# Another order of tokens, ring loads split around a loop's test, and an expert's odd-shaped matmuls gathered into one run

## The chip, the cores and the metric

One core of one Trainium2 chip runs the whole program. The metric is device time in microseconds (us) of one execution. The core has a matmul engine (PE, whose weight loads are listed as PEld), two elementwise engines (DVE and ACT), a general engine (POOL, idle here), and a sequencer (SP) that issues nearly all transfers. ACT issues a few. All transfers run on the same 16 DMA engines.

## The reference, cut to what matters

Two layers over 256 tokens of 1024 float32 values. Each layer mixes tokens in four branches (neighbourhood attention on a 4 x 64 grid, differential attention, pooling, dilated attention), and then sends each token to 2 of 32 experts:

```python
h = layer_norm(x, emb_ln_g, emb_ln_b)
for l in range(2):
    z = h @ w_in[l]                                  # 1024 x 8192 weights
    ... four branches, gates, merged @ w_out[l] ...
    h = layer_norm(ALPHA * h + mix, ln1_g[l], ln1_b[l])
    # group by argmax, then the top 2 of 8 experts in the group
    # expert e: (silu(t @ w_gate[e]) * (t @ w_up[e])) @ w_down[e], weighted by its gate
    h = layer_norm(ALPHA * h + ffn, ln2_g[l], ln2_b[l])
return h                                             # (1, 256, 1024)
```

An expert's three matrices are 2 MB each. All 32 are read in each layer, 201 MB, whether tokens chose them or not.

## The kernel before, in words

**Tokens.** The kernel keeps the 256 tokens in an order of its own, on two tiles of 128 partitions. Slot `64r + 16b + a` holds token `16a + 4b + r`, so that tokens with the same remainder by 4 lie together, as the dilated branch wants. `x` comes in with four transfers of 64 rows of 4 KB (line 390), and the result leaves with four such transfers, two issued by SP and two by ACT (line 1009). The rows of one transfer are walked as 4 x 16. The neighbourhood branch needs the plain order, so lines 617, 618, 623, 638 and 652 (its `y_store`) read or write through two views, `grid` and `mine`.

**Weights.** `weight_sources` names the blocks of weights in the order in which they are used, and `load_weight` issues the next one whenever a buffer of 1 MB comes free. There are eight buffers that live all through (`rawp`), eight that open with the third branch (`rawb`), and four (`rawc`, the ring) that open with `open_ring` after the output projection, in the room of the tiles `wh` and `wl`. A block of `w_in` that is made of two column ranges of 256 is filled by two transfers per buffer, with pieces of 1 KB; one that is 512 columns wide by one transfer, with pieces of 2 KB.

**Token mixing.** Each weight block is split by ACT (`high`, line 233) and DVE (`low`, line 238) into two parts, and PE makes three passes over them (lines 447, 466 and 759). At the start the program loads `x`, takes its mean and variance (lines 259 to 275), normalises it (290, 292), turns it on PE (346), and scales it by columns of gains (298, 300) that come from two small loads (306), turned on PE (315) and copied by ACT (316). Then the first products begin.

**Experts.** After routing, `overflow` tests whether any expert has more than 64 tokens: every engine loads the number of trips (line 1301) and passes a loop (1302) that runs zero times here. Then the loop of `moe` over 32 experts `p` has twelve steps `s`. Steps 0 to 7 multiply the tokens of expert `p` by its gate and up matrices (843), and free two buffers each at s = 3 and s = 7. Steps 8 to 11 are the down product of expert `p - 1` (867), which frees one buffer at s = 9 and one at s = 11. Beside them, by the table `STEPS`: `combine` adds expert `p - 2` to the sum (888), `turn` transposes the hidden values (853). For the next batch of four experts, `gather` picks token rows by matmul (803), one piece at s = 5 and one at s = 6, and `gathered` copies them out (812). `gather_meta` (820) does the same for token numbers once in four experts. The order of the instructions inside this loop is as written (`manual_schedule`). Outside of such a block, a scheduler decides where an instruction stands on its engine.

**End.** After the last expert the second sum is normalised (259, 999, 1006) and written out (1009).

Of the kernel before, what the change touches and what calls it, by code (L numbers as in the profile page):

```python
# [29 lines left out]
G = 2  # L30
NORM_ON = ((1, 0), (1, 0))
RAW = (4, 2, 4, 4)

STEPS = ((0, 2, "select"), (3, 2, "combine"), (7, 0, "evacuate"), (9, 0, "turn"), (9, 0, "silu"), (9, 0, "times_up"),
         (11, 1, "weigh"))


def token_order():
    p = np.arange(SEQ)
    r, b, a = p // 64, (p // 16) % 4, p % 16  # L40
    return 16 * a + 4 * b + r

# [64 lines left out]
class Kernel:  # L107
# [19 lines left out]
    def open_ring(self):  # L127

        self.close_side()
        self.side = [self.tc.tile_pool(name=f"rawc{self.layer}", bufs=RAW[2] * 2 // G, side="right", reuse_waits="tile")]  # L130
        self.rawc, = (p.__enter__() for p in self.side)
        for _ in range(RAW[2] * 2 // G):
            self.load_weight(self.rawc)
# [11 lines left out]
    def weight_sources(self):  # L145
        a = self.a
        for l in range(self.depth):
# [3 lines left out]
            def cols(*starts, w=w):  # L151
                return [(w[:, :, s:s + 256], 256) for s in starts]

            yield l, [(w[:, :, d:d + 512], 512)]
            yield l, cols(d + 768, d + 1024)
            yield l, cols(d + 1536, d + 1792)
            yield l, cols(d + 512, d + 1280)
# [212 lines left out]
    def run(self):  # L370
        tc, nc, a = self.tc, self.nc, self.a
        with ExitStack() as ctx:
# [14 lines left out]
            h = self.new_h()  # L387
            x = a["x"].rearrange("o (a b r) d -> r b (o a) d", b=4, r=4)
            for r in range(4):
# [43 lines left out]
    def mixing(self, l):  # L433
# [37 lines left out]
        with ExitStack() as ctx:  # L471
# [144 lines left out]

            grid = lambda t: t.rearrange("p (a b r) -> p r b a", b=4, r=4)
            mine = lambda t: t.rearrange("p (r b a) -> p r b a", r=4, b=4)
            ps = crosswise()
# [157 lines left out]
    def moe(self, l):  # L777
        tc, nc, a, c = self.tc, self.nc, self.a, self.c
        mm, t2, t4, t8 = self.mm, self.t2, self.t4, self.t8
        with ExitStack() as ctx:  # L780
# [48 lines left out]
            with tc.tile_pool(name=f"route{l}", bufs=1) as rp:  # L829
                with tc.manual_schedule():  # L830
                    router, xh, xl, acc = self.output_and_route(l, rp, route, meta, slots, gather, gathered)
                self.overflow(l, rp, route, *router, xh, xl, acc)
                gates = router[1]
            work = pool("mwork", 2)
# [59 lines left out]
            with tc.manual_schedule():  # L894
                nc.vector.tensor_copy(meta[:, :, :, 1], gates)
                for p in range(N_EXP):
# [4 lines left out]
                    for s in range(12):  # L901
# [8 lines left out]
                        if p == 0 and s in (1, 3):  # L910
# [3 lines left out]
                            gathered(0, s // 2 + 2, ps, s == 1)  # L914
                        if j == 0 and s == 8:
                            gather_meta(b0, gb)
                            gathered_meta(b0, gb)
                        if e0 < N_EXP and s in (5, 6):
                            gather(e0, 2 * j + s - 5, gb, xh, xl)
                            if s == 6:  # L920
                                gathered(e0, j, gb, False)
                        if s < 8:
                            i = s // 4 * 2
                            products(p, s, tiles[i][:, s % 4], tiles[i + 1][:, s % 4])
                            if s % 4 == 3:
                                free(i)
                                free(i + 1)
                        elif p:
                            down(p - 1, s - 8, tiles[s // 2 - 4][:, s % 2], dn)
                            if s % 2:  # L930
                                free(s // 2 - 4)
                        for at, lag, f in STEPS:
                            if at == s and p >= lag:
                                steps[f](p - lag)
# [58 lines left out]
                else:  # L993
# [8 lines left out]
                    mv = self.norm_stats(0, 1, meanwhile=first)  # L1002
                    o = self.out.rearrange("o (a b r) d -> r b (o a) d", b=4, r=4)
                    for T in range(2):
# [385 lines left out]
```

## Time and profile before

| What | Value |
|---|---|
| median of 3 runs | 1569.12 us (1568.67 to 1569.28) |
| the profiled execution, its own time | 1568.56 us |
| its span | 1566.4 us |
| PE busy | 1486.1 us, 95% |
| DVE, ACT busy | 574.2 us, 465.3 us |
| moved by DMA | 501.14 MB, mean 320 GB/s |
| mixing, layer 0 and layer 1 | about 30 to 303 us, and 791 to 1066 us |
| experts, layer 0 and layer 1 | about 325 to 784 us, and 1085 to 1542 us |

The span is the stretch in which instructions were recorded; 2.2 us of the profiled execution lie outside of it. [...] What a change is worth must be read stage by stage: in the mixing stages PE hardly rests while the DMA engines are partly idle, and in the expert stages the DMA engines are busy without a gap.

### The profile page before, as it was taken

To read this page: it belongs to the slowest core of one execution; us is meant where nothing else is said; L and a number is where in the kernel's file an instruction comes from. 1 tells how busy PE (TensorE), PEld (TensorE's weight loads), DVE (VectorE), ACT (ScalarE), POOL (GpSimd) and SP (SyncE) were. 2 spreads that over 40 slices of the span, in tenths; PEclk is the share of its full clock that TensorE was granted. 3 is DMA by queue.
4 is the path that set the end of the run, shared out by engine and by line. 5 is a ranking of instruction groups with operands and counts; after the bars stand their busy time and mean duration, and the time that the engine had idled before them with its cause. 6 is when DMAs were issued, how large, how long until landed. Compare 5 with 4: busy or idle time off the path is not lost. (4 is left out here: it accounts for less than half of the span.)

```text
span 1566.4 us, 21436 instructions
## 1 busy us (share of the span) xinstructions
PE 1486.1 (95%) x8776; PEld 863.4 (55%) x8776; DVE 574.2 (37%) x1202; ACT 465.3 (30%) x756; POOL 0.2 (0%) x4
## 2 busy tenths in 40 slices
PE   3999999989999999999989999999999999999993
PEld 2787799843334333334468778996333333333342
DVE  3676675721111111111176776664111111111113
ACT  3545554521111111111165455454111111111111
POOL 0000000000000000000000000000000000000000
PEclk9999999999999999999999999999999999999997
DMA  8773386569999999999998246754999999999993
GB/s 221 210 281 108 111 302 207 199 230 420 420 420 419 419 421 419 420 419 420 394 268 287 91 133 209 249 179 187 412 420 420 419 420 421 419 419 421 420 420 124
DMA packets 125785, 501.14 MB, mean 320 GB/s; under 512 B 23082, under 2 KB 44010, under 8 KB 76788
## 3 DMA queue, kind: packets, MB, share of 16 engines
q1 hardware_dynamic: 125400, 499.14, 82.5%
q8 instruction: 71, 1.16, 0.3%
q10 hardware_dynamic: 284, 0.60, 0.1%
q14 instruction: 30, 0.25, 0.0%
HBM read 498.65 MB, written 2.00 MB: 320 GB/s over the span
## 5 line engine op out<-in xcount | busy, mean ns | idle before, releaser
L843 PE MATMUL bank<-raw,xs 128*64 128x512 f32 x2048 | 496.4, 603 | 12.8 <-SPq L1302 5.3
L843 PEld LDWEIGHTS bank<-raw,xs 128*64 128x64 f32 x2048 | 138.5, 136 | 239.2 <-issue 201.5
L867 PE MATMUL bank<-raw,act 128*64 128x512 f32 (+1 forms) x1056 | 247.2, 586 | 0.0
L847 ACT COPY hid<-bank 128x512 f32<-128x512 f32 x64 | 68.4, 1069 | 582.3 <-PE bank L843 582.3
L238 DVE TENSOR_TENSOR wl<-raw,wh 128x1024 fp32r<-128x1024 f32 x160 | 193.7, 1221 | 109.5 <-ACT wh L233 107.9
L233 ACT CAST wh<-raw 128x1024 fp32r<-128x1024 f32 x160 | 166.5, 1048 | 139.1 <-PE mm L466 63.7
L812 DVE COPY xs<-bank 128x256 f32<-128x256 f32 x116 | 43.8, 419 | 343.2 <-PE bank L803 343.2
L466 PE MATMUL mm<-hth,wl 128*128 128x256 f32 x576 | 162.6, 283 | 1.6 <-DVE wl L238 1.6
L466 PE MATMUL mm<-hth,wh 128*128 128x256 f32 x576 | 162.8, 283 | 0.2 <-ACT wh L233 0.2
L466 PE MATMUL mm<-htl,wh 128*128 128x256 f32 x576 | 162.3, 282 | 0.0
L867 PEld LDWEIGHTS bank<-raw,act 128*64 128x64 f32 x1056 | 74.2, 137 | 107.7 <-issue 101.0
L862 DVE TENSOR_TENSOR act<-act,bank 128x256 f32<-128x256 f32 x64 | 27.0, 421 | 265.6 <-ACT act L859 265.6
L466 PEld LDWEIGHTS mm<-hth,wl 128*128 128x128 f32 x576 | 109.2, 190 | 3.1 <-DVE wl L238 1.8
L466 PEld LDWEIGHTS mm<-hth,wh 128*128 128x128 f32 x576 | 109.2, 190 | 2.5 <-issue 2.0
L466 PEld LDWEIGHTS mm<-htl,wh 128*128 128x128 f32 x576 | 109.6, 190 | 0.8 <-issue 0.7
L879 DVE SCALAR_TENSOR_TENSOR y<-bank,tg,y 128x512 fp32r<-128x512 f32 (+1 forms) x66 | 48.5, 735 | 115.4 <-ACT y L878 115.4
L803 PEld LDWEIGHTS bank<-g,xh 128*128 128x128 f32 x240 | 36.2, 190 | 94.9 <-issue 94.9
L447 PE MATMUL mm<-wh,hth 128*128 128x512 f32 x224 | 75.7, 409 | 2.0 <-DVE t L300 1.0
L878 ACT ACTIVATE y<-bank,tg 128x512 fp32r<-128x512 f32 (+1 forms) x66 | 44.5, 674 | 100.5 <-PE bank L867 100.5
L447 PE MATMUL mm<-wl,hth 128*128 128x512 f32 x224 | 73.2, 405 | 0.0
L447 PE MATMUL mm<-wh,htl 128*128 128x512 f32 x224 | 71.5, 401 | 0.0
L803 PE MATMUL bank<-g,xh 128*128 128x256 f32 x240 | 60.7, 335 | 0.0
(220 smaller groups left out, 1420.6 us busy)
## 6 DMA issues: line engine op xcount, KB each, us to landing
raw<-in_expert_w_gate_dram SPq DMA_DIRECT2D x128, 1024.0 KB, 18.2
raw<-in_expert_w_up_dram SPq DMA_DIRECT2D x128, 1024.0 KB, 19.9
raw<-in_expert_w_down_dram SPq DMA_DIRECT2D x124, 1024.0 KB, 19.7
raw<-in_w_in_dram SPq DMA_DIRECT2D x48, 1024.0 KB, 7.5
raw<-in_w_in_dram SPq DMA_DIRECT2D x32, 512.0 KB, 8.7
raw<-in_w_branch_dram SPq DMA_DIRECT2D x8, 1024.0 KB, 4.9
raw<-in_w_out_dram SPq DMA_DIRECT2D x8, 1024.0 KB
raw<-in_expert_w_down_dram SPq DMA_DIRECT2D x16, 256.0 KB, 8.3
```

What stands on the lines that cost most here:

```text
L233: self.nc.scalar.copy(hi, s)
L238: self.nc.vector.tensor_sub(lo, s, raw(hi))
L447: nc.tensor.matmul(ps[T], s[:, kk, T * 128:(T + 1) * 128], m[:, k], stop=kk == 7 and s is stat[1], start=kk == 0 and s is stat[0] and m is wh)
L466: nc.tensor.matmul(ps[j // 2][:, j % 2], m[:, k, j * 128:(j + 1) * 128], s[:, kk], start=j % 2 == 0 and kk == 0 and m is wh and s is hth, ...
L803: nc.tensor.matmul(ps[:, o:o + 256], (xh, xl)[i][:, T, k], gs[e0][:, T], start=i == 0 and T == 0, stop=i == 1 and T == 1)
L812: (nc.scalar.copy if on_scalar else nc.vector.tensor_copy)(xs[e0 + 2 * i][:, :, 2 * j:2 * j + 2], ps[:, 2 * i:2 * i + 2])
L843: nc.tensor.matmul(gu[half[i]], x, w, start=k == 0, stop=k == 7)
L847: nc.scalar.copy(st["h", e].rearrange("q (h k p) -> q h p k", h=2, k=2), gu.rearrange("q (h p k) -> q h p k", h=2, k=2))
L862: nc.vector.tensor_mul(st["a", e], st["a", e], fv[:, :, 1])
L867: nc.tensor.matmul(ps[half[f], :w.shape[2]], st["a", e][:, k], w[:, f], start=k == 0, stop=k == 3)
L878: nc.scalar.activation(yh, ps, AF.Copy, scale=g)
L879: nc.vector.scalar_tensor_tensor(yl, ps, g, raw(yh), op0=ALU.mult, op1=ALU.subtract)
```

## The change

Four edits:

1. Slot `64r + m` now holds token `4m + r`. Each transfer of `x` and of the result is walked as 64 rows. `grid` and `mine` become views of two dimensions, r and m, in place of three.
2. Two blocks of `w_in` per layer, which were two adjacent ranges of 256 columns, are now written as one of 512.
3. `open_ring` fills two of the ring's four buffers, and `load_ring` is called again after the overflow loop for the other two.
4. In the expert loop, both gathers move to s = 9, after the down product of that step; `combine` moves from s = 3 to s = 9, after `turn`; `gather_meta` moves from s = 8 to s = 6.

```diff
-STEPS = ((0, 2, "select"), (3, 2, "combine"), (7, 0, "evacuate"), (9, 0, "turn"), (9, 0, "silu"), (9, 0, "times_up"),
+STEPS = ((0, 2, "select"), (7, 0, "evacuate"), (9, 0, "turn"), (9, 0, "silu"), (9, 0, "times_up"), (9, 2, "combine"),
          (11, 1, "weigh"))
 def token_order():
     p = np.arange(SEQ)
-    r, b, a = p // 64, (p // 16) % 4, p % 16
-    return 16 * a + 4 * b + r
+    return 4 * (p % 64) + p // 64
...
-        for _ in range(RAW[2] * 2 // G):
+        self.load_ring()
+
+    def load_ring(self):
+
+        for _ in range(RAW[2] // G):
             self.load_weight(self.rawc)
...
-            yield l, cols(d + 768, d + 1024)
-            yield l, cols(d + 1536, d + 1792)
+            yield l, [(w[:, :, d + 768:d + 1280], 512)]
+            yield l, [(w[:, :, d + 1536:d + 2048], 512)]
...
-            x = a["x"].rearrange("o (a b r) d -> r b (o a) d", b=4, r=4)
+            x = a["x"].rearrange("o (m r) d -> r (o m) d", r=4)
...
-            grid = lambda t: t.rearrange("p (a b r) -> p r b a", b=4, r=4)
-            mine = lambda t: t.rearrange("p (r b a) -> p r b a", r=4, b=4)
+            grid = lambda t: t.rearrange("p (m r) -> p r m", r=4)
+            mine = lambda t: t.rearrange("p (r m) -> p r m", r=4)
...
                 self.overflow(l, rp, route, *router, xh, xl, acc)
+                self.load_ring()
...
-                        if j == 0 and s == 8:
+                        if j == 0 and s == 6:
                             gather_meta(b0, gb)
                             gathered_meta(b0, gb)
-                        if e0 < N_EXP and s in (5, 6):
-                            gather(e0, 2 * j + s - 5, gb, xh, xl)
-                            if s == 6:
-                                gathered(e0, j, gb, False)
...
+                        if e0 < N_EXP and s == 9:
+                            for k in range(2):
+                                gather(e0, 2 * j + k, gb, xh, xl)
+                            gathered(e0, j, gb, False)
...
-                    o = self.out.rearrange("o (a b r) d -> r b (o a) d", b=4, r=4)
+                    o = self.out.rearrange("o (m r) d -> r (o m) d", r=4)
```

What the four edits move on the engines can be seen in the built programs. The first place is the start of SP's queue, before and then now; the size behind a transfer is the shape that it is walked in.

```order
L390 DMA h<-in_x_dram 64x1x1024 x4
L215 DMA raw<-in_w_in_dram 128x4x512 x2
L407 DMA cs<-in_const_small_dram 128x898
L215 DMA raw<-in_w_in_dram 128x4x256 x12
L417 DMA rpb_141<-in_na_rpb_dram 64x1860
```

```order
L394 DMA h<-in_x_dram 64x1024 x4
L219 DMA raw<-in_w_in_dram 128x4x512 x2
L411 DMA cs<-in_const_small_dram 128x898
L219 DMA raw<-in_w_in_dram 128x4x512 x4
L219 DMA raw<-in_w_in_dram 128x4x256 x4
L421 DMA rpb_137<-in_na_rpb_dram 64x1860
```

The rows of `x` lost an inner dimension, and eight transfers of 256 columns became four of 512. Nothing changed places.

The second place is SP's queue around the loop's test in layer 0, before and then now, with the buffers' numbers, which follow the order in which the code asks for them (`tripsi` is the number of trips).

```order
L197 DMA raw_3044<-in_expert_w_gate_dram 128x2048
L197 DMA raw_3046<-in_expert_w_up_dram 128x2048
L200 DMA raw_3048<-in_expert_w_down_dram 128x2048
L200 DMA raw_3050<-in_expert_w_down_dram 128x2048
L1301 TENSOR_LOAD tripsi_3227
L1301 ISA x2
L1019 DMA rw_5955<-in_router_group_w_dram 128x8x4
L1302 COMPARE_AND_BRANCH
```

```order
L201 DMA raw_3040<-in_expert_w_gate_dram 128x2048
L201 DMA raw_3042<-in_expert_w_up_dram 128x2048
L204 DMA raw_3393<-in_expert_w_down_dram 128x2048
L204 DMA raw_3395<-in_expert_w_down_dram 128x2048
L1306 TENSOR_LOAD tripsi_3219
L1306 ISA x2
L1024 DMA rw_5947<-in_router_group_w_dram 128x8x4
L1307 COMPARE_AND_BRANCH
```

The two loads that are now asked for behind the loop (3393 and 3395, numbers above that of `tripsi`) still stand ahead of the test on SP: the scheduler put them there. The same holds in layer 1.

The third place is PE at the last expert of a layer, before and then now: `raw,xs` are the gate and up products, `raw,act` the down products, `cs,hid` the transposes, `y,sel` the combining.

```order
L843 MATMUL bank<-raw,xs 64x512 x8
L888 MATMUL at<-y,sel 128x512 x4
L888 MATMUL mm<-y,sel 128x512 x4
L843 MATMUL bank<-raw,xs 64x512 x8
L867 MATMUL bank<-raw,act 64x512 x4
L853 MATMUL bank<-cs,hid 128x128 x4
L867 MATMUL bank<-raw,act 64x512 x4
```

```order
L848 MATMUL bank<-raw,xs 64x512 x16
L872 MATMUL bank<-raw,act 64x512 x4
L858 MATMUL bank<-cs,hid 128x128 x4
L893 MATMUL at<-y,sel 128x512 x4
L893 MATMUL mm<-y,sel 128x512 x4
L872 MATMUL bank<-raw,act 64x512 x4
```

The eight matmuls of `combine` moved from the middle of the gate and up products to a place behind all of them, next to the transposes. In earlier experts the gathers stand there too.

## Rows read from the trace of the kernel before

**Rows 1.** The page: GB/s moved, in 40 equal slices of the span.

```profile
GB/s 221 210 281 108 111 302 207 199 230 420 420 420 419 419 421 419 420 419 420 394 268 287 91 133 209 249 179 187 412 420 420 419 420 421 419 419 421 420 420 124
```

**Rows 2.** Windows: length, engines' busy us (instructions), clock, DMA share, GB/s.

```profile
333.00:345.00 12.00, 11.74 (x88) 5.22 (x84) 1.34 (x4) 1.45 (x2) 0.00 (x0) 1.00 0.92 354
...
400.00:450.00 50.00, 50.00 (x271) 19.44 (x270) 8.16 (x20) 7.49 (x10) 0.00 (x0) 1.00 1.01 420
...
1092.00:1480.00 388.00, 387.74 (x2080) 151.10 (x2081) 64.43 (x155) 58.95 (x83) 0.00 (x0) 1.00 1.01 418
```

**Rows 3.** Chain of waits, steady experts of layer 1: start us, us, what.

```profile
1110.70 3.43 PE bank L843 x16
...
1167.52 3.43 PE bank L843 x16
```

**Rows 4.** Chain of waits, last expert of layer 1.

```profile
1502.77 19.86 DMA raw<-in_expert_w_up_dram
...
1522.67 3.65 PE bank L843 x14
1526.32 0.66 PE at L888 x4
1526.98 0.47 PE mm L888 x4
1527.45 3.84 PE bank L843 x16
```

**Rows 5.** Timeline of the start: start us, us, engine, line, operation, [idle before, releaser].

```profile
0.73 2.49 SPq L390 DMA_DIRECT2D h<-in_x_dram  x4
...
3.26 3.18 SPq L215 DMA_DIRECT2D raw<-in_w_in_dram  x2
...
9.43 0.98 PE L315 MATMUL mm<-cs,rows 2*128 2x2 f32 x8 [9.43 <-DMA rows<-in_emb_ln_b_dram]
...
13.98 1.29 DVE L259 BATCH_NORM_STATS2 st<-h 128x6 f32<-128x512 f32 x2 [10.39 <-DMA h<-in_x_dram]
...
22.13 1.29 DVE L259 BATCH_NORM_STATS2 st<-h 128x6 f32<-128x512 f32 x2 [6.86 <-DMA h<-in_x_dram]
...
23.56 0.48 ACT L270 ACTIVATE w<-mv,eps 128x1 f32<-128x1 f32 x2 [12.94 <-DVE mv L269]
...
25.87 3.67 PE L346 MATMUL mm<-cs,h 128*128 128x128 f32 x16 [15.45 <-ACT h L290]
26.42 1.03 ACT L233 CAST wh<-raw 128x1024 fp32r<-128x1024 f32 x1
...
30.40 1.22 PE L447 MATMUL mm<-wh,hth 128*128 128x512 f32 x2 [0.86 <-DVE t L300]
```

**Rows 6.** Windows of the start.

```profile
6.00:8.00 2.00, 0.00 (x0) 0.00 (x0) 0.00 (x0) 0.00 (x0) 0.00 (x0) 1.00 1.04 239
...
24.00:26.00 2.00, 0.13 (x1) 0.14 (x2) 1.98 (x10) 1.04 (x3) 0.00 (x0) 1.00 0.36 117
```

**Rows 7.** DMA issues of the first 6 us: KB each, median us to landing.

```profile
raw<-in_w_in_dram SPq DMA_DIRECT2D x2, 1024.0 KB, 21.2
```

**Rows 8.** Timeline of the end.

```profile
1548.57 2.73 DVE L1006 SCALAR_TENSOR_TENSOR h<-h,mv,ln 128x512 f32<-128x512 f32 x4
1550.00 1.90 SPq L1009 DMA_DIRECT2D out_dram<-h  x2
```

**Rows 9.** Windows: the output, and the stretch around the loop's test in layer 0.

```profile
1557.00:1563.00 6.00, 0.00 (x0) 0.00 (x0) 0.00 (x0) 0.00 (x0) 0.00 (x0) 0.50 0.25 104
...
318.00:333.00 15.00, 9.73 (x49) 5.70 (x50) 3.35 (x20) 1.94 (x6) 0.00 (x0) 0.77 0.12 15
```

**Rows 10.** Timeline: PE's first expert matmul, SP's first load behind it, ACT's table.

```profile
325.12 1.98 PE L843 MATMUL bank<-raw,xs 128*64 128x512 f32 x4 [5.27 <-SPq L1302]
...
333.06 0.33 SPq L197 DMA_DIRECT2D raw<-in_expert_w_gate_dram  x1
...
819.46 1.28 ACT L497 ACT_TABLE_LOAD   x1
```

## The prediction

> **What bounds the kernel now.** I read the page first, for where the transfers are slow: two plateaus at 420 GB/s, about 200 GB/s between them, and poor slices at both ends [rows 1]. The windows then say what each plateau is: over 388 us of layer 1's experts the DMA engines are busy all the time at 418 GB/s, and PE is marked busy as well [rows 2]. Which of the two decides is told by the chain of waits. In the steady stretch four experts take PE 1167.52 - 1110.70 = 56.8 us, 14.2 us each [rows 3]. Their weights, 6.29 MB each, take 6.29 / 0.420 = 15.0 us. So PE is 0.8 us per expert faster than its supply. It lives on filled buffers and runs dry at the end: the chain there is a transfer of 19.86 us, then PE [rows 4]. In the expert stages the end is therefore set by when the transfers began to run without a gap, by the bytes left then, and by PE's work behind the last piece. The mixing stages are the other way round: the reader sees it in the DMA engines' half-idle slices, so whatever delays PE's first product there delays everything behind it.
>
> Next the start. The second half of x arrives at 22.13, and everything on DVE, ACT and PE up to the first product at 30.40 waits for it [rows 5]. The DMA engines are not idle then, but they do little: full share at 239 GB/s at 6 to 8 us, and at 24 to 26 us only 0.36 of them are in use [rows 6]. The first weights, issued at 3.26, take 21.2 us to land, so they too come at 24.5 [rows 7]. At the end, DVE has written the result at 1548.57 + 2.73 = 1551.3, and SP has issued its last transfer at 1551.9 [rows 8], but the span ends at 1566.4. In most of the 14.5 us between, 0.25 of the DMA engines are busy, which is 4 of 16, at 104 GB/s [rows 9]. The result is walked as 4 x 16 rows there: the number of engines in use is the outer count, 4. The same holds for x, whose rows are those of the same pattern.
>
> **The change part by part.** *End.* With 64 as the outer count, which 16 divides, I take the result's transfers to use all 16 engines. Its 1.05 MB at 104 GB/s are 10.1 us, at the 420 GB/s of the plateau 2.5 us: 7.6 us less, and this is the small end, since it leaves the slow first microseconds as they are. The large end lets 3.5 us stand between the last issue and the end of the span, 11 less. Before 1557 the rate is below 104, so that part shrinks too; I take -10.
>
> [...]
>
> *Start.* x is 1.05 MB as well, and its four issues end at 3.22. At 420 GB/s it has landed at 5.7, at the 239 GB/s of that stretch at 7.6. With something for the landing I take 7, against 22.13: 15.1 us earlier. One thing can bind before that. ACT copies the gain columns ahead of its square root in its queue, and PE turns them at 9.43 for 0.98 us; if they come as late as now, the square root of 23.56 cannot start before 10.65, and 12.9 us are left. These two small loads share engines with x's rows, so they should come earlier too. And the first weights must be there for the cast of 26.42, which would be due at 11.3: x and the first megabyte behind it, 2.1 MB from 3.2 us on, land at 8.2 by 420 and at 12.0 by 239 GB/s. So I take -14.5, between -11.9 and -16.4. Behind it PE needs half a megabyte per 2.8 us (12 matmuls of two 128-row tiles), which is less than either rate, so the shift should pass to the end of the mixing stage, and from there, through the first freed buffers, to the experts' transfers.
>
> *The experts' runs.* Breaking a run of one shape costs PE something, and three or more breaks per expert go. That makes PE faster in stages in which its supply sets the end, so it is worth nothing there: PE waits longer for the last pieces. What it may bring is at the front of each expert stage, before the transfers run without a gap: 354 GB/s in the first 12 us against 420, which is 1.9 us per layer [rows 2], most of it the delay of the very first transfer. The first freed buffers hang on s = 3, where nothing changes, the next on s = 7, which comes earlier by two gathers and later by the token-number gather. I take -0.5 per layer (0 to -1.9).
>
> At the last expert the move costs something. `combine` stands now behind the first half of the gate and up products and takes 1527.45 - 1526.32 = 1.13 us [rows 4]. The second half's weights come 5 us behind the piece that ended PE's wait at 1522.67, so about 1527.6: there PE would have to wait anyway. At s = 9 it stands on PE's path to the end, with all waits behind it: +1.1 per layer, +2.2 together (0 to 2.4).
>
> *The ring.* In the built program the two loads stand on SP ahead of the test, as before: nothing, then. If they did go out behind it, this is the cover: the DMA engines do 15 GB/s between 318 and 333 [rows 9]; PE starts at 325.12, and SP's next load waits for PE until 333.06 [rows 10], so two megabytes (5 us) fit in between. In layer 1 that gap is tighter: 0 to 1 us. PE's wait of 5.27 us at the test stays, as the small router load still stands between test and loop.
>
> *Weights of 512 columns.* Eight loads of 1 MB go out as one transfer each, not two. They are in stages where PE sets the pace: 0. If it moves the time, it is by the start's first weights, within the bounds above.
>
> *Order of ACT in layer 1.* The scheduler now puts a table load (1.28 us) and an exponential ahead of two copies that PE waits for [rows 10]: +0.5, from -0.5 to +1.3. The two-dimensional views leave the same elements in the same instructions: 0.
>
> **Sum.** -10 - 14.5 - 1.0 + 2.2 + 0.5 = -22.8, on the profiled execution's 1568.56: 1545.8. The median of the runs is 0.56 above that execution, so 1546.3, and I forecast 1546.
>
> **The rivals.** *Rows of 64 partitions are slower than a plateau's rate.* The plateau's transfers fill 128 partitions, those of x and the result 64. If such transfers run at half the plateau's rate, 210 GB/s, x lands at 8.2 (1.2 later) and the result takes 2.5 us more: about 1550. For it: the start's transfers do run at 239 and less at full share. Against it: weights of 128 partitions are among those.
>
> [...] No row here shows a transfer of 64 partitions that is wide enough to tell.
>
> *The start gains less.* x comes early, but the gain columns or the first weights stay late; the first product then moves by 8, not 14.5: 1553. For it: the weights' 239 GB/s may be that stretch's own slowness, not x's.
>
> *The transfers do not spread.* If the outer count is not what gives 4 engines, both ends stay, and the rest is -1.0 + 2.2 + 0.5: 1571, no measurable change. Against it: 0.25 is sharp, and the result is the one transfer in flight.
>
> *The run at s = 9 makes PE the slower one.* Gathers, transposes and combining now follow one another behind a copy by ACT, and stand ahead of the down product that frees a buffer at s = 11. If PE's expert grew from 14.2 to more than 15.0 us, each further microsecond would cost about 60 us over both layers; from 15.4 us on it eats the gain of both ends. At 16.0: 1546 + 60 = 1606, slower. Against it: no instruction is added, and fewer breaks stand in the run.
>
> **How the numbers follow.** Forecast 0.67 (its own range 1541 to 1549), half-rate rows 0.18, a start that gains less 0.07, no spread 0.05, PE slower 0.03. Range: the low end adds the large ends of both gains to most of the first stretch's, 1541; the high end takes in the half-rate rows and most of the third case, 1553. A measurement of this kernel tells about 0.2% (3 us) from no change. Faster by more than that: 0.92, within 0.05, slower 0.03.
>
> **What would show it.** In the profile after: x's second half ends DVE's wait at 6 to 9 us, and the first product starts near 16; the DMA share in the output is near 1, and the span ends 4 to 7 us after the last issue; PE's waits in both expert stages begin earlier and last longer, while the transfers still run at 420 GB/s; `combine` follows the transposes at the last expert, 1.1 us on PE. It is wrong if the output still shows 0.25, if the first product stays behind 20 us, or if the plateaus have gaps.

## The result and the profile after

The changed kernel took 1549.43 us (median of 4, 1545.67 to 1554.07), the kernel before 1569.20 us beside it: a ratio of 0.9876 (95% interval 0.9857 to 0.9896). Measured again later, in 6 executions against 10 of the kernel before, it was 1547.55 us and 0.9852 (0.9824 to 0.9880). The forecast was 1546 us, the range 1541 to 1553. The profiled execution took 1549.12 us with a span of 1547.0 us, 19.4 less than before.

**The plateaus.** The page's row of GB/s, which answers [rows 1]:

```profile
GB/s 331 233 185 113 147 313 191 192 268 419 420 420 419 420 419 420 419 420 420 381 262 279 103 137 182 258 179 185 402 420 420 420 419 419 421 419 421 419 420 222
```

Two plateaus at 420 GB/s as before; the first slice has gone from 221 to 331 GB/s.

**The start.** The timeline, which answers [rows 5] (start us, us, engine, line, operation, [idle before, releaser]):

```profile
5.99 1.28 DVE L263 BATCH_NORM_STATS2 st<-h 128x6 f32<-128x512 f32 x2 [2.23 <-DMA h<-in_x_dram]
8.16 1.28 DVE L263 BATCH_NORM_STATS2 st<-h 128x6 f32<-128x512 f32 x2 [0.88 <-DMA h<-in_x_dram]
...
9.59 0.48 ACT L274 ACTIVATE w<-mv,eps 128x1 f32<-128x1 f32 x2 [2.60 <-DVE mv L273]
...
16.42 1.22 PE L451 MATMUL mm<-wh,hth 128*128 128x512 f32 x2 [0.86 <-DVE t L304]
```

And windows of it, which answer [rows 6] (length, engines' busy us, clock, DMA share, GB/s):

```profile
4.00:6.00 2.00, 0.20 (x2) 0.23 (x3) 0.01 (x1) 0.00 (x0) 0.00 (x0) 1.00 1.05 242
6.00:8.00 2.00, 0.78 (x8) 0.69 (x7) 1.28 (x2) 0.17 (x1) 0.00 (x0) 1.00 0.99 226
8.00:10.00 2.00, 0.00 (x0) 0.00 (x0) 1.80 (x7) 0.41 (x2) 0.00 (x0) 1.00 1.05 390
```

x's second half ends DVE's wait at 8.16 (before: 22.13), and the first product starts at 16.42 (before: 30.40). All engines are in use from the start (DMA share 0.97 between 2 and 4 us, 0.99 to 1.05 behind it), but they reach 390 GB/s only when x is there.

**The end.** Timeline and windows, which answer [rows 8, 9]:

```profile
1538.75 2.73 DVE L1011 SCALAR_TENSOR_TENSOR h<-h,mv,ln 128x512 f32<-128x512 f32 x4
1540.18 1.82 SPq L1014 DMA_DIRECT2D out_dram<-h  x2
```

```profile
1542.00:1543.00 1.00, 0.00 (x0) 0.00 (x0) 0.00 (x0) 0.00 (x0) 0.00 (x0) 0.50 0.99 213
...
1544.00:1545.00 1.00, 0.00 (x0) 0.00 (x0) 0.00 (x0) 0.00 (x0) 0.00 (x0) 0.50 0.93 344
```

The share is near 1 where it was 0.25, and the span ends 5.0 us behind SP's last issue (1542.0), not 14.5.

**Between the ends.** The two gains are 14.0 and 9.5 us, 23.5 together, but the span is only 19.4 shorter. Where the rest went is read by setting the same event of both timelines side by side, and the kernel with the first edit alone (below) beside them:

| Event | before, us | changed | first edit alone |
|---|---|---|---|
| first product on PE | 30.40 | -13.98 | -13.90 |
| SP's first ring load, layer 0 | 305.46 | -13.49 | -13.76 |
| first expert product, layer 0 | 325.12 | -13.14 | -13.54 |
| SP's first load behind it | 333.06 | -11.83 | -13.30 |
| last transposes of layer 0's experts | 774.86 | -10.41 | -13.88 |
| layer 1's first transposes | 790.05 | -9.33 | -13.87 |
| first expert product, layer 1 | 1084.71 | -10.69 | -13.59 |
| SP's first load behind it | 1090.98 | -10.69 | -13.59 |
| last transposes of layer 1's experts | 1533.01 | -10.89 | -14.14 |
| DVE's write of the result | 1548.57 | -9.82 | -14.14 |
| end of the span | 1566.4 | -19.4 | -23.8 |

The changed kernel loses 0.8 us between its first product and its first expert product, 1.3 at layer 0's test, 1.4 in that layer's expert stage, and 1.1 behind the last expert of each layer, and wins 1.4 back in layer 1's mixing. Not all of it need be the edits' doing. In the fourteen profiles of this document, whatever the kernel, an expert stage took 440.8 to 443.6 us from SP's first load behind its first product to its last transposes (before 441.8, changed 443.2, changed and run again 442.0 in layer 0). With the old order of the expert loop it was 441.2 to 442.0, with the new one 440.8 to 443.6.

**The loop's test.** Timeline of the changed kernel, then its windows, which answer [rows 9, 10]:

```profile
311.98 1.98 PE L848 MATMUL bank<-raw,xs 128*64 128x512 f32 x4 [5.63 <-SPq L1307]
...
321.23 0.33 SPq L201 DMA_DIRECT2D raw<-in_expert_w_gate_dram  x1
```

```profile
311.50:316.50 5.00, 4.52 (x14) 2.37 (x16) 0.76 (x2) 0.50 (x2) 0.00 (x0) 0.51 0.21 31
316.50:321.50 5.00, 5.00 (x24) 2.01 (x22) 0.76 (x2) 0.14 (x1) 0.00 (x0) 0.81 0.01 2
```

And windows of the kernel before:

```profile
319.50:324.50 5.00, 0.35 (x3) 0.15 (x2) 0.33 (x3) 0.73 (x3) 0.00 (x0) 0.74 0.13 8
325.00:330.00 5.00, 4.88 (x18) 2.56 (x20) 0.76 (x2) 0.65 (x2) 0.00 (x0) 0.62 0.22 33
330.00:335.00 5.00, 5.00 (x30) 2.23 (x24) 0.76 (x2) 0.00 (x0) 0.00 (x0) 1.00 0.17 26
```

The granted clock (third number from the right) falls in both kernels. Before, about half of that fell into PE's wait, where it costs nothing, and full speed was back by 330. Now nearly all of it lies on the first expert's products.

**The expert loop.** The group of the gate and up products, of the changed kernel and then of the kernel before (busy us, mean ns, idle before and its releasers):

```profile
L848 PE MATMUL bank<-raw,xs 128*64 128x512 f32 x2048 | 493.0, 597 | 33.6 <-DMA raw<-in_expert_w_up_dram 25.4 <-SPq L1307 5.6 <-issue 2.4
```

```profile
L843 PE MATMUL bank<-raw,xs 128*64 128x512 f32 x2048 | 496.4, 603 | 12.8 <-SPq L1302 5.3 <-DMA raw<-in_expert_w_up_dram 5.2 <-issue 2.4
```

In this group PE waits 25.4 us for weights, five times as long as before. Two experts that follow each other start their products 13.2 us apart while the buffers are full (before: 14.2, [rows 3]):

```profile
339.48 7.04 PE L848 MATMUL bank<-raw,xs 128*64 128x512 f32 x32
...
352.64 7.04 PE L848 MATMUL bank<-raw,xs 128*64 128x512 f32 x32
```

And the chain of waits at the last expert, which answers [rows 4]:

```profile
1496.85 19.86 DMA raw<-in_expert_w_up_dram
...
1516.75 3.22 PE bank L848 x13
...
1520.40 1.72 PE bank L872 x7
1522.12 0.59 PE bank L858 x4
1522.70 0.67 PE at L893 x4
1523.37 0.46 PE mm L893 x4
1523.84 1.89 PE bank L872 x8
```

PE's wait now is for the second half of the weights, and `combine` (1.13 us) lies behind it.

### The profile page after: what moved, and what is told of

It is laid out like the page before. It is cut to its first block, busy times and chain, and to the rows that moved or that the text cites. A ratio compares the mean times of both kernels' runs of the same rounds, so it can differ in the third digit from the quotient of the medians.

```text
span 1547.0 us, 21415 instructions
## 1 busy us (share of the span) xinstructions
PE 1470.3 (95%) x8776; PEld 896.8 (58%) x8776; DVE 574.3 (37%) x1202; ACT 465.3 (30%) x756; POOL 0.2 (0%) x4
## 5 line engine op out<-in xcount | busy, mean ns | idle before, releaser
L848 PE MATMUL bank<-raw,xs 128*64 128x512 f32 x2048 | 493.0, 597 | 33.6 <-DMA raw<-in_expert_w_up_dram 25.4
L848 PEld LDWEIGHTS bank<-raw,xs 128*64 128x64 f32 x2048 | 174.6, 137 | 314.7 <-issue 232.1
L872 PE MATMUL bank<-raw,act 128*64 128x512 f32 (+1 forms) x1056 | 266.4, 585 | 0.0
L872 PEld LDWEIGHTS bank<-raw,act 128*64 128x64 f32 x1056 | 81.3, 136 | 131.1 <-issue 123.7
L864 ACT ACTIVATE act<-bank 128x256 f32<-128x256 f32 x64 | 24.6, 384 | 128.0 <-PE bank L858 125.8
## 6 DMA issues: line engine op xcount, KB each, us to landing
raw<-in_expert_w_gate_dram SPq DMA_DIRECT2D x128, 1024.0 KB, 19.9
raw<-in_expert_w_up_dram SPq DMA_DIRECT2D x128, 1024.0 KB, 19.9
raw<-in_expert_w_down_dram SPq DMA_DIRECT2D x124, 1024.0 KB, 19.9
```

The lines of the kernel that those rows point to most:

```text
L848: nc.tensor.matmul(gu[half[i]], x, w, start=k == 0, stop=k == 7)
L872: nc.tensor.matmul(ps[half[f], :w.shape[2]], st["a", e][:, k], w[:, f], start=k == 0, stop=k == 3)
```

## The experiments

**1. The first edit alone**, in the kernel before.

```diff
-    r, b, a = p // 64, (p // 16) % 4, p % 16
-    return 16 * a + 4 * b + r
+    return 4 * (p % 64) + p // 64
...
-            x = a["x"].rearrange("o (a b r) d -> r b (o a) d", b=4, r=4)
+            x = a["x"].rearrange("o (m r) d -> r (o m) d", r=4)
...
```

> The kernel before with the first edit alone (order of tokens, 64 rows as the outer dimension of x and of the result). Theory 1: the whole gain is at the two ends, and the third of it that went missing between the first product (14.0 us earlier) and layer 0's expert transfers (11.6 earlier) went into PE's clock, which comes back later behind the wait at the loop's test, whatever the expert loop's order. Then the first product starts near 16.4 us, the span ends 5 us behind the last issue, the time is 1546 to 1549 us (up to 2.1 below the changed kernel, which pays `combine` at the last expert of two layers), and the loss of about 2 us at layer 0's test appears here too if the granted clock is low while PE works on its first expert matmuls, and doesn't if the clock was low only during the wait. Rival: the loss comes from the expert loop's new order. Then layer 0's expert transfers keep the full 13.5 us here, whatever the clock did, and the time is 1544 to 1546.

Measured: 1542.6 us (6 runs) against 1567.62, ratio 0.9843 (0.9819 to 0.9867). The table above has its profile: the 14 us of the start are kept to the end. The ratio makes 1544.6 of 1569.2, nearer to the rival's number, but the interval spans both. At the test 0.2 us were lost, with the clock low on PE's first products. I had expected some 2 us for that case, and had not set it against the kernel before, whose clock was low there too; the table behind experiment 4 does.

**2. The fourth edit alone**, in the kernel before.

```diff
-STEPS = ((0, 2, "select"), (3, 2, "combine"), (7, 0, "evacuate"), ...
+STEPS = ((0, 2, "select"), (7, 0, "evacuate"), ..., (9, 2, "combine"),
...
-                        if j == 0 and s == 8:
+                        if j == 0 and s == 6:
...
+                        if e0 < N_EXP and s == 9:
...
```

> The kernel before with the fourth edit alone (gathers and `combine` at s = 9). Theory 1: PE becomes about 1 us per expert faster, its waits grow, the transfers set the end as before, and `combine` adds 1.1 us behind the last weights of each layer: 1569.2 + 2.1 = 1571.3 us, and layer 0's expert transfers start when they did before (0, within 0.5 us, if the clock falls at the same place). Rival: the new order delays the first freed buffers by 2 us per layer: 1569.2 + 2.1 + 4 = 1575. A third way, on the other side: a faster PE brings the first transfers forward by up to 1.9 us per layer: 1567.5.

Measured: 1571.5 us (12 runs) against 1567.62, ratio 1.0024 (1.0007 to 1.0041): slower, so the third way is out. The interval takes in theory 1's 2.1 us and, at its edge, the rival's 6. The profile decides: SP's first load in layer 0 stands 8.05 us behind the first expert product, where it was 7.94 in the kernel before, not 2 us later. In layer 1 it was 7.84 against 6.27, with the clock low:

```profile
1090.53:1098.53 8.00, 8.00 (x34) 3.96 (x36) 1.32 (x4) 0.65 (x2) 0.00 (x0) 0.79 0.00 1
```

**3. `combine` back at s = 3**, in the changed kernel.

```diff
-STEPS = ((0, 2, "select"), (7, 0, "evacuate"), ..., (9, 2, "combine"),
+STEPS = ((0, 2, "select"), (3, 2, "combine"), (7, 0, "evacuate"), ...
```

> The changed kernel with `combine` back at s = 3, the gathers left at s = 9. Theory 1: `combine` lies in PE's wait for the second half of the last gate and up weights, as it did before, and the time from the last landing of those weights to the end shrinks by 1.1 us in each layer: 1549.4 - 2.1 = 1547.3 us. Rival: the 1.1 us are hidden again by another wait on that path (ACT's or DVE's work between the down products): 1549.4, the same.

Measured: 1543.19 us (5 runs), ratio 0.9853 (0.9829 to 0.9877). The chain of waits at the last expert of layer 1:

```profile
1506.94 3.65 PE bank L848 x14
1510.59 0.66 PE at L893 x4
1511.25 0.47 PE mm L893 x4
1511.72 3.85 PE bank L848 x16
1515.58 1.72 PE bank L872 x8
1517.29 0.59 PE bank L858 x4
1517.88 1.89 PE bank L872 x8
```

From the end of the gate and up products to the second half of the down products it is 1517.88 - 1515.58 = 2.3 us here, and 1523.84 - 1520.40 = 3.4 in the changed kernel. All fourteen profiles say the same: from layer 0's last transposes to layer 1's first it is 15.2 us in the six with `combine` at s = 3 and 16.3 in the eight with it at s = 9. And it costs nothing at s = 3: the last `up` weights are issued at 1492.02 here and at 1496.85 in the changed kernel, so with the 19.9 us that such a transfer takes to land, the transposes follow the landing by 5.4 us in both. So `combine` costs 1.1 us per layer at s = 9 and nothing at s = 3. The total is 4 us below theory 1's, and the changed kernel measured again (experiment 12) has the same ratio: the totals can't tell 2 us.

**4. The second and third edits alone**, in the kernel before.

```diff
-            yield l, cols(d + 768, d + 1024)
+            yield l, [(w[:, :, d + 768:d + 1280], 512)]
...
                 self.overflow(l, rp, route, *router, xh, xl, acc)
+                self.load_ring()
```

> The kernel before with the second and third edits alone (two blocks of w_in in pieces of 2 KB, the ring's loads asked for in two places). Theory 1: nothing: 1569.2, within 2 us, and PE's pace in the branches (113 or 118 ns for a product of 256 columns) is not changed by them. Rival: the 3 us that layer 1's branches were faster in the changed kernel come from these loads; then 1566, with the pace at 113 ns from about 950 us on.

Measured: 1567.91 us (12 runs) against 1567.62, ratio 1.0011 (0.9997 to 1.0026): nothing. The pace of the branches' products is the new thing in its profile. Windows of it in layer 0 and layer 1, 20 us each (x is the number of products):

```profile
240.00:260.00 20.00, 20.00 (x172) 20.00 (x172) 12.98 (x15) 9.78 (x14) 0.00 (x0) 1.00 0.45 161
960.00:980.00 20.00, 20.00 (x179) 20.00 (x178) 14.47 (x22) 12.19 (x17) 0.00 (x0) 1.00 0.86 294
```

The same of the kernel before, and then of the changed kernel:

```profile
240.00:260.00 20.00, 20.00 (x179) 20.00 (x178) 13.91 (x16) 9.42 (x13) 0.00 (x0) 1.00 0.48 168
960.00:980.00 20.00, 20.00 (x172) 20.00 (x172) 12.96 (x19) 12.13 (x18) 0.00 (x0) 1.00 0.83 283
```

```profile
952.00:972.00 20.00, 20.00 (x179) 20.00 (x178) 13.61 (x21) 12.61 (x18) 0.00 (x0) 1.00 0.85 292
```

There are two paces, 172 and 179 products of 256 columns in 20 us, at the full clock in both. Over the 97 us that they last in a layer it makes 4%, some 3 to 4 us. The edits alone don't set it: in layer 0 the changed kernel had 179 in one profile and 172 in another (experiment 12), and in layer 1 two of the eleven kernels with these two edits are slow, which differ from the changed kernel in x's load alone. But the three kernels without them are all fast in layer 0 and slow in layer 1, where those with them are fast in six and in nine of eleven. So whether the two edits make a pace likelier stays open. The total shows no gain from it. The 1.4 us that the changed kernel won in layer 1's mixing are, as I read it, what is left of the pace there, since its clock was low for a while in the same stretch (0.86 between 930 and 940 us).

**The clock at the test, from several profiles.** To decide between the two theories of experiment 1, the mean granted clock of the 8 us behind the first expert product is set against the time from that product to SP's first load:

| Kernel, layer | clock in 8 us | us to SP's first load |
|---|---|---|
| changed, layer 0 | 0.60 | 9.25 |
| outer count 8 (below), 0 | 0.62 | 9.05 |
| first edit alone, 0 | 0.73 | 8.18 |
| fourth edit alone, 0 | 0.75 | 8.05 |
| before, 0 | 0.77 | 7.94 |
| `combine` back, 0 | 0.79 | 7.83 |
| fourth edit alone, layer 1 | 0.79 | 7.84 |
| before, changed, first edit alone, 1 | 1.00 | 6.27 |

The old and the new order of the expert loop lie on one line, and the stages that are not in the table fit it (0.64 with 8.93, 0.75 to 0.81 with 8.08 to 7.68, 1.00 with 6.26 to 6.28). So what was lost at the test is the clock, which theory 1 said: it fell at another place against PE's wait. Where it falls isn't set by the edits, since the changed kernel run again had 0.78 and 7.92 there.

**5. Filled waits.** `combine` at s = 3, and products that nothing reads in PE's three waits.

```diff
...
+    def idle(self, bank, n):
+        two = self.ones[:, None, :].to_broadcast([128, 2, 128])
+        for _ in range(n):
+            self.nc.tensor.matmul(bank[:, :256], self.ones, two, start=True, stop=True)
...
+                self.idle(self.mm.tile([128, 512], F32, tag="mm", name="idle"), 22)
...
+            self.idle(bank(), 44)
...
+                    self.idle(turned, 46)
```

> The changed kernel with `combine` back at s = 3, and with products that nothing reads put into PE's waits: 22 of 256 columns ahead of the first transposes, 44 ahead of each loop's test, 46 ahead of layer 1's transposes. Theory 1 (PE's clock falls because of these waits, and comes back when PE has worked for a while): the granted clock stays high at layer 0's test, SP's first expert load follows PE's first expert product by 6.3 us (7.8 to 9.3 us in the five profiles in which the clock was low there, 6.3 where it was not), and layer 1's first products run at 0.23 us per 512 columns from the start. That is 1.6 to 3 us at the test, about 1.5 between the layers and 1 to 3 at the start: 4 to 7 us under the kernel without the filling, 1537 to 1539 by the runs so far. Rival: the products only push back what waits in PE's queue, and the clock falls all the same (it fell for 3.4 us in the middle of the branches too, where PE hardly waits): the same time, 1543, or up to 2 us more.

Measured: 1547.57 us (6 runs), ratio 0.9889 (0.9865 to 0.9913): not faster than experiment 3. Its windows and its timeline at layer 0's test:

```profile
311.48:319.48 8.00, 8.00 (x49) 3.82 (x49) 1.40 (x4) 0.65 (x2) 0.00 (x0) 1.00 0.10 14
```

```profile
317.75 0.33 SPq L201 DMA_DIRECT2D raw<-in_expert_w_gate_dram  x1
```

The clock held, and the first load came 317.75 - 311.48 = 6.27 us behind the first product, as theory 1 said. But the loop opened later: against experiment 3, DVE's wait at it grew from 5.60 to 6.86 us in layer 0, where the clock's 1.6 us were won, and from 2.19 to 5.66 in layer 1, where experiment 3 had lost nothing to the clock (6.28 us to SP's first load). That took more than was won. I put both down to the number of products, which PE had to pass before it came to the test.

**6. Filled less.** 30 products ahead of layer 0's test, none ahead of layer 1's.

```diff
-            self.idle(bank(), 44)
+            if l == 0:
+                self.idle(bank(), 30)
```

> As the kernel with filled waits, but with 30 products ahead of layer 0's test in place of 44, and none ahead of layer 1's. There the filling itself was late: PE came to the test 5.5 us after its last gather, and the loop opened 1.65 us behind PE, so 1.3 us later than without in layer 0 and about 3.5 us in layer 1, where the wait had been only 2.3 us. Theory: with those two losses gone the time is below the kernel with `combine` at s = 3 and nothing filled (1543.2 us, ratio to before 0.985): the clock at the test (1.6 us), between the layers (0.7) and at the start (1) give 1540. Rival: 30 products leave 1.5 us of wait, the clock falls all the same, and the time is 1543.

Measured: 1549.85 us (6 runs), ratio 0.9877 (0.9849 to 0.9904). My theory fell. DVE's wait at the test, in the timeline:

```profile
314.89 0.76 DVE L804 TENSOR_TENSOR g<-route,cs 128x256 fp32r<-128x256 f32 x2 [6.86 <-SPq L1317]
```

In layer 0 it is 6.86 us with 30 products as with 44, so their number is not the reason. What moves the loop's opening there stays open; in both kernels SP issues the last three router loads ahead of the test, which it did behind it without the filling. In layer 1 the number had been the reason, since DVE's wait there is 2.20 us with none and was 5.66 for PE with 44. But the loss came all the same, as PE's first product followed 3.0 us behind DVE:

```profile
1069.09 0.76 DVE L804 TENSOR_TENSOR g<-route,cs 128x256 fp32r<-128x256 f32 x2 [2.20 <-SPq L1317]
...
1072.11 1.12 PE L854 MATMUL bank<-raw,xs 128*64 128x512 f32 x2 [5.20 <-issue]
```

PE waited for nothing that this view shows. Without the filling that gap was 0.2 us. The chain of waits names no releaser for it either: behind DVE's writes of `g` it has 2.25 us of "issue", from 1069.86 to 1072.11. What held PE there stays open.

**7. and 8. Outer counts of 8 and of 16**, in the changed kernel (8 shown).

```diff
-    return 4 * (p % 64) + p // 64
+    return 32 * (p % 8) + 4 * (p // 8 % 8) + p // 64
...
-            x = a["x"].rearrange("o (m r) d -> r (o m) d", r=4)
+            x = a["x"].rearrange("o (a b r) d -> r b (o a) d", b=8, r=4)
...
```

> The changed kernel with rows of x and of the result walked as 8 x 8, between the 4 x 16 of before and the 64 of now. Theory 1: the outer count is the number of DMA engines a transfer uses. Then 8 engines carry x and the result: the result at twice the 104 GB/s of before takes 5.0 us, 2.5 of the 5.0 between last issue and end become about 9.4 us (0.50 of the DMA engines busy there), and x's second half lands half way, near 12 to 13 us; the first product 4 us later than now, near 20.5. Rival: any outer count above 4 spreads over all 16; then 8.2 us, 16.4 us and 5.0 us as now.

Measured: 1553.89 us (one run). Timeline and windows:

```profile
13.55 1.28 DVE L263 BATCH_NORM_STATS2 st<-h 128x6 f32<-128x512 f32 x2 [3.57 <-DMA h<-in_x_dram]
```

```profile
10.00:12.00 2.00, 0.00 (x0) 0.00 (x0) 0.00 (x0) 0.11 (x1) 0.00 (x0) 1.00 1.04 168
...
14.00:16.00 2.00, 0.00 (x0) 0.00 (x0) 1.94 (x11) 0.48 (x2) 0.00 (x0) 1.00 1.05 394
...
1543.00:1545.00 2.00, 0.00 (x0) 0.00 (x0) 0.00 (x0) 0.00 (x0) 0.00 (x0) 0.50 0.49 115
```

> The changed kernel with rows of x and of the result walked as 16 x 4. Theory 1: 16 engines, as with 64: x's second half at 8.2 us, the first product at 16.4, the span ends 5.0 us behind the last issue, all within 0.5. Rival: what counts is that a transfer is one plain list of 64 rows; then 16 x 4 stays closer to the 4 x 16 of before than to now, with x later than 12 us.

Measured: 1546.98 us (one run).

With 8, the share is 0.49 at the end, the span ends 9.8 us behind SP's last issue, and x is there at 13.55. With 16 it is 4.6 us and 8.32, as with 64. So in these runs the number of engines in use was the outer count, up to 16: the share in the output is 0.25 with 4, 0.49 with 8 and 0.93 to 0.99 with 64, and with 16 the times are those of 64.

**9. x from two queues**, in the changed kernel.

```diff
-                nc.sync.dma_start(h[r // 2][(r % 2) * 64:(r % 2) * 64 + 64], x[r])
+                (nc.sync, nc.scalar)[r % 2].dma_start(h[r // 2][(r % 2) * 64:(r % 2) * 64 + 64], x[r])
```

> The changed kernel with x's four transfers issued in turn by SP and by ACT, so that rows for the lower and for the upper 64 partitions are under way at the same time. Theory 1 (a transfer of 64 rows to half of the partitions moves at about half the plateau's rate, the third of the rivals on record): both halves together move at up to 390 GB/s as the weights behind them do, and x's second half lands near 6 us in place of 8.16, the first product near 14.5. Rival: the first microseconds are slow whatever is moved; then 219 to 242 GB/s stay until x is there, and it lands at 8.2 as now. (The gain columns are issued later by ACT here, and stay hidden up to about 9 us.)

Measured: 1550.63 us (one run). The timeline and a window:

```profile
8.26 1.29 DVE L263 BATCH_NORM_STATS2 st<-h 128x6 f32<-128x512 f32 x2 [1.12 <-DMA h<-in_x_dram]
```

```profile
6.00:8.00 2.00, 0.00 (x0) 0.00 (x0) 1.13 (x2) 0.00 (x0) 0.00 (x0) 1.00 0.97 226
```

Nothing gained: theory 1 as I had put it fell. The rival fell too, in experiment 7, where the rate stayed at 168 to 293 GB/s between 6 and 14 us, until x was there at 13.55, so the slowness goes with x and not with the first microseconds.

**10. Rows that follow each other.**

```diff
-            x = a["x"].rearrange("o (m r) d -> r (o m) d", r=4)
+            x = a["x"].rearrange("o (r m) d -> r (o m) d", r=4)
```

> The changed kernel, but each of x's four transfers reads 64 rows that follow each other in memory, in place of every fourth row (so the tokens are not in the order that the rest takes them to be in, and the result is that of other tokens). Theory 1: x's rows take 272 ns each, against 159 ns for the result's rows of the same 4 KB and for other loads of 4 KB later on, because they lie 16 KB apart; then x's second half lands near 6 us here, the DMA engines move over 350 GB/s between 2 and 6 us, and the first product is at 14.5. Rival: it is x's first reading, or the first microseconds, whatever the distance of the rows; then 219 to 242 GB/s and 8.2 us as now.

Measured: 1544.83 us (one run); a window:

```profile
4.00:6.00 2.00, 0.12 (x2) 0.15 (x2) 0.00 (x0) 0.00 (x0) 0.00 (x0) 1.00 1.03 225
```

x at 8.31. How far apart the rows lie is not the reason.

**11. x in transfers of 128 rows.**

```diff
-            x = a["x"].rearrange("o (m r) d -> r (o m) d", r=4)
-            for r in range(4):
-                nc.sync.dma_start(h[r // 2][(r % 2) * 64:(r % 2) * 64 + 64], x[r])
+            x = a["x"].rearrange("o (t m) d -> t (o m) d", t=2)
+            for r in range(2):
+                nc.sync.dma_start(h[r], x[r])
```

> x read as two transfers of 128 rows that follow each other in memory, in place of four of 64 (the tokens are in another order than the rest takes them to be in, so the result is that of other tokens). Left open so far: x's rows move at 225 to 242 GB/s with all 16 engines in use, whether they lie apart in memory or not, and whether they fill one half of the partitions or both from two queues; the rate goes to 384 to 394 GB/s as soon as x is there. Theory 1: a transfer of 64 rows is slow as such; then 128 rows move at over 350 GB/s, x's second half lands near 6 us and the first product is near 14.5. Rival: reading x is slow however it is cut; then 8.2 and 16.4 us as with four transfers.

Measured: 1546.85 us (one run). The timeline and windows:

```profile
5.59 2.46 DVE L263 BATCH_NORM_STATS2 st<-h 128x6 f32<-128x512 f32 x4
```

```profile
4.00:6.00 2.00, 0.00 (x0) 0.00 (x0) 0.55 (x2) 0.00 (x0) 0.00 (x0) 1.00 0.99 340
6.00:8.00 2.00, 0.98 (x8) 0.92 (x8) 2.00 (x5) 0.00 (x0) 0.00 (x0) 1.00 1.04 392
```

DVE no longer waits between the halves, and the first product starts at 15.03. So reading x is not slow however it is cut: transfers of 64 rows to 64 partitions are slow (219 to 256 GB/s), and two of them side by side from two queues do not make up for it (226 to 244). These transfers are also twice as large (0.5 MB), and no run separates that from the 128 partitions.

**12. The changed kernel once more.**

> The changed kernel itself, once more, beside the others. Theory 1: its runs differ among themselves by as much as 8 us (1545.7 to 1554.1 so far) because PE's clock falls at other places from run to run, and because the pace of the branches' products is 113 or 118 ns from about the third branch of a layer on; a profile of it will show another pair of those than the first (113 ns in both layers, 3.4 us of low clock in layer 1's branches, 6.4 us of low clock on the first expert), and its median lies 3 to 5 us above the kernel with the first edit alone: a ratio of 0.987 to before. Rival: the 3 to 5 us between them are these differences alone, and the ratio is 0.985, as with the first edit alone.

Measured: 1547.55 us (6 runs, 1542.87 to 1552.84), ratio 0.9852 (0.9824 to 0.9880). The profile had another pair of paces (172 and 179, the first profile 179 in both layers) and low clock on layer 1's first expert:

```profile
1074.77:1082.77 8.00, 8.00 (x34) 4.05 (x36) 1.31 (x4) 0.65 (x2) 0.00 (x0) 0.79 0.00 1
```

Another pair, as theory 1 said. Its ratio is the rival's: by totals, the changed kernel and the first edit alone (0.9843) can't be told apart here. That the first edit alone is some 2 us faster rests on the chains of waits, not on the totals. The 3 to 5 us of theory 1 did not come.

## Why the prediction was right, and where not

*End, -10.* Right: -9.5. That a transfer walked as 64 rows uses all 16 engines was taken there without a run that showed it; the share of 0.93 to 0.99 in the output shows it. The small end would have been 7.6. The transfers of the result also run at 213 GB/s in their first microsecond, so its data takes longer than 2.5 us.

*Start, -14.5.* Right in size: -14.0. The landing of x was mis-sized, 8.16 against the 7 that I took. The low bound of -11.9 is not what its terms give, -12.9 from the gain columns. The first of the rivals (experiment 9's expectation calls it the third) named this number, 8.2, and its reason, transfers of 64 rows at about half rate (219 to 256 GB/s, against 420), is borne out by experiment 11, with size and partitions not separated. I had set it aside because weights of 128 partitions move in the same slow stretch. They do, but only while x's rows are under way: in experiment 7 the rate was 168 to 293 GB/s until x was there and 394 behind it. All 16 engines were in use there (share 0.99 to 1.05 from 6 us on), and by the outer count only 8 of them for x (0.49 in the output), so the weights were slowed in engines without x's rows as well. Why stays open. The rival's second price did not come: the result lost only 0.5 against my term.

*The experts' runs.* The mechanism was right: PE 1.0 us per expert faster (13.2 against 14.2), its waits five times as long, the plateaus at 420 GB/s, the end unmoved. The fear that PE becomes the slower one had no ground. The gain at the front was the step that failed: -0.5 per layer, of a range of 0 to -1.9, was +1.3 in layer 0 (SP's first load) and 0 in layer 1. Nothing in my working looked at the clock, though the row of the kernel before showed 0.77 between 318 and 333 [rows 9]. With 6.27 to 9.25 us up to SP's first load, against 7.94 before, 1.7 us less or 1.3 more than before were possible there, and the second lay outside of my bounds. What the new order itself brought was 0.7 us behind that first load: the second pair of loads came 325.60 - 321.23 = 4.4 us after it, and 338.13 - 333.06 = 5.1 before. At the end of the stages no gain shows (440.8 to 443.6 us, against 441.2 to 442.0 with the old order).

*`combine`, +1.1 per layer.* Right: 1.08 and 1.07 in the table, none with `combine` back at s = 3. Before, it lay in the wait for the second half.

*Ring, weights of 512 columns: 0.* Right: the medians are 0.3 us apart, and the interval of the ratio, -0.5 to +4.1 us, takes in 0 (experiment 4).

*ACT's order in layer 1, +0.5.* It was +0.3. From layer 1's first transposes to the first product of line 466 (470 in the changed kernel) it is 65.7 us in the kernel before, with the first edit alone and with `combine` back at s = 3, and 66.0 in the changed kernel. So this comes with `combine` at s = 9.

*What no term had.* The changed kernel lost 0.8 us of its start up to the first expert product, and 1.4 in layer 0's expert stage. That lies within the stage's spread; what causes the spread stays open. It won 1.4 in layer 1's mixing, by the pace. These nearly cancel. Of 22.8 us predicted 19.4 came. The 3.4 between are 0.9 at both ends together, 1.8 + 0.5 at the two first stretches against what I took, and the rest of these small terms.

*Luck.* That 1546 and 1549 lie so close is in part luck. In the fourteen profiles an expert stage differs by almost 3 us, layer 0's mixing takes 273.5 to 277.5 us (first product to the ring's loads), and layer 1's 291.4 to 296.9 (first transposes to first expert product; the longest is experiment 5's, with its filling). Neither the pace nor the clock was in the sum.

*How far a measurement tells.* 0.2% was about right for the interval of some runs, not for one run: the kernel before took 1562.15 to 1578.46 us in 49 executions.

## What to carry to other kernels

Count the engines of a transfer by its outer dimension (4 of them in use at 4 here, 8 at 8, 16 at 64), and look at both ends of a kernel, where nothing hides a transfer: here that was the whole gain. Fill 128 partitions with one transfer where you can; x's transfers of 64 rows ran at 219 to 256 GB/s with all 16 engines in use, whatever queue they came from, and with two transfers of 128 rows, twice as large, the rate was 340 between 4 and 6 us. In a stage that its supply bounds, look only at what stands behind the last piece: work that is moved out of the wait for it is paid in full (`combine`, 1.1 us per layer), and a faster engine is paid nothing (PE, 1.0 us per expert). Before a shift of 14 us at the start is carried through to the end, look what lies beside it that is not set by the program, here the place where the clock falls.

## What the runs showed of the hardware

- In eleven profiles without filling PE's granted clock was low behind its wait at layer 0's test (5.27 us in the kernel before): a mean of 0.60 to 0.79 over the 8 us behind the first product, at a place that shifts from run to run. Behind layer 1's (2.4 us) it was 0.79 to 0.81 in four of them and 1.00 in the other seven. It also fell without such a wait: in the changed kernel it was 0.50 between 930 and 932 us, with PE busy all the time and no wait over 0.52 us in the 5 us before. Work of the first expert up to SP's first load took 6.27 us at full clock and 9.25 at a mean of 0.60.
- The same products ran at two paces at full clock, 172 or 179 in 20 us, over whole stretches of a layer. What chooses between them stays open.
- x's 64-row transfers kept all 16 engines busy (share 0.89 to 1.05) at 219 to 256 GB/s; once x was there, the next transfers ran at 379 to 394.
